# Diagonal blocks gathered by ScalarE, and one 128-partition block transpose in place of four, in a recurrence's inverse

## The chip, the cores and the metric

The kernel runs on one core of a Trainium2 chip. The metric is device time in microseconds of one execution. Six kinds of rows appear in its profile: PE and PEld (TensorE's matmuls and weight loads), DVE (VectorE), ACT (ScalarE), POOL (GpSimd) and SP (the engine that issues most DMAs). Each engine works through its own queue in order; an instruction whose inputs are not ready holds up everything behind it on that engine.

## The reference

One layer of a hybrid model over 2048 tokens of width 1024, with 256 context tokens ahead of them, in float32: a norm with modulation, a projection to 4544 columns, two token mixers over those columns, an output projection, and a layer of 16 experts. The mixer that matters here is RWKV-7, run forwards and backwards over 8 heads of 64:

```python
def step(S, inp):
    r_t, w_t, k_t, v_t, a_t, b_t = inp
    sa = jnp.einsum('bhvk,bhk->bhv', S, a_t)
    S = S * w_t[:, :, None, :] + sa[..., None] * b_t[:, :, None, :] + v_t[..., None] * k_t[:, :, None, :]
    return S, jnp.einsum('bhvk,bhk->bhv', S, r_t)
```

The other mixer is a retention with a fixed decay; its columns are the projection `h @ w_in` over the first 2560 columns.

## The kernel before

The kernel does not walk the recurrence token by token. It cuts the tokens into chunks of 64. Inside a chunk the term `sa` of each token depends on those of the tokens before it; written out, that is a triangular system of 64 by 64 per head and chunk, whose inverse is needed. A `Job` is 256 tokens (four chunks, 8 heads) in one direction: 9 blocks times 2 directions are 18 jobs, forward and backward in turn.

How a job goes, by the names in the code:

- `loads`, `decays`, `decays_b` fetch its rows and multiply in the running decays (DVE and ACT).
- `product(m, q)`, four times: matmuls on PE into PSUM (`pA`), and DVE multiplies by a mask into `ab` (the triangular matrices) and `rb`. Partitions 0 to 63 of `ab` hold one half of the chunks (q = 0), 64 to 127 the other (q = 1); the free axis has 16 matrices of 64 columns for each q.
- `corners(q)` (lines 970 to 980): each 64 by 64 triangle is seen as two 32 by 32 diagonal blocks and one corner block. ACT copies the corner into `lo`; DVE transposes the diagonal blocks into `xp`. A DVE block transpose turns each 32 by 32 block by itself, so what lies on one partition as (16 matrices, 32 columns) comes out with the matrix index along the free axis. There is one transpose per diagonal block, each of 32 partitions and 1024 elements (every element is written twice, by a broadcast).
- `inverses`: POOL inverts all the 32 by 32 blocks at once by back substitution, 31 steps of a multiply (line 997) and an add (line 1000) on `dm`.
- `spread(q)` (lines 1002 to 1010): DVE transposes the inverted blocks back, from `dm` into the two diagonal places of `Y[d]`, and one of the two once more into `Dn` (tile `D` in the profile).
- `solve`: matmuls in eight steps. Its third step multiplies `lo` by `Dn` and ACT copies the product over the other half of `Dn`; its fourth multiplies that by `y` and ACT copies it into the corner of `y`; the later steps apply `y`.
- `chain`: the four chunks one after the other, each with a matmul into `pC`, a DVE add into `uv`, a matmul, a DVE add and multiply into the next state `z`, and matmuls for the outputs (`yo`).

The order is written out by hand: every matmul, DVE and ACT instruction of this stage keeps its program order. The loop of lines 1186 to 1203 has 12 slots per job. In slot i it issues one step of the chain of the job before, then a share of the retention columns' matmuls as filler (`fill_slot`, 9.1 per slot; 24 of them make one column tile in the single PSUM bank `pr`, which ACT then reads into `ru`), then the steps of the job's own solve (its third and fourth are in slots 6 and 7), and last what is prepared for it or for the next job: `product` of the next job in slots 4 to 7, `corners` of the next job in slot 7, `inverses` from slot 8 to its slot 16, and `spread` in slot 17, that is in slot 5 of the job's own turn. POOL also issues the column loads `rh` in the same queue as the inverses; SP issues the other loads.

`xp`, `lo`, `D`, `ab` and `dm` have one buffer each. Nearly all instructions carry line 126 in the profile (the helper that records them), so the rows below go by tile names; `hi` in a row of this stage is another name on the same memory (the decays, the masks).

Of the kernel before, what the change touches and what calls it, by code (L numbers as in the profile page):

```python
# [8 lines left out]
F32 = mybir.dt.float32  # L9
# [75 lines left out]
def body(ctx: ExitStack, tc, a, out, scratch, stop=None, only=None):  # L85
# [53 lines left out]
    vec, act, pool = Ordered(nc.vector), Ordered(nc.scalar), Ordered(nc.gpsimd)  # L139
# [728 lines left out]
    def rwkv():  # L868
        with ExitStack() as es:
            one = es.enter_context(tc.tile_pool(name="s1", bufs=1, reuse_waits="tile"))  # L870
# [6 lines left out]
            Dn = one.tile([128, 16, 32], F32, name="D")  # L877
# [28 lines left out]
            class Job:  # L906
# [62 lines left out]

                def corners(self, q):  # L970

                    if "xp" not in self.__dict__:
                        self.xp = one.tile([128, 1024], F32, name="xp")
                        self.lo = one.tile([128, 16, 32], F32, name="lo")
                    r, b = slice(64 * q + 32 * self.d, 64 * q + 32 * self.d + 32), 32 - 32 * self.d
                    act.copy(out=self.lo[r], in_=self.ab[r, q].rearrange("p m h t -> p (m h) t")[:, :, b:b + 32])
                    for b in range(2):
                        r = slice(64 * q + 32 * b, 64 * q + 32 * b + 32)
                        src = self.ab[r, q].rearrange("p m h (y t) -> p y t (m h)", y=2)[:, b]
                        vec.transpose(out=self.xp[r], in_=self.rev(src)[:, :, None, :].to_broadcast([32, 32, 2, 16]))  # L980

                def inverses(self, j0, j1):

# [15 lines left out]
                            tc.keep_in_program_order(x)  # L999
                        eng.tensor_add(dm[:, 0:j, j // 2:], dm[:, 0:j, j // 2:], tv)  # L1000

                def spread(self, q):

                    d, y = self.d, Y[self.d]
                    dm = self.dm.rearrange("p (s r) -> p r s", r=16)
                    for b in (1 - d, d):
                        r, t = slice(64 * q + 32 * b, 64 * q + 32 * b + 32), slice(32 * b, 32 * b + 32)
                        o = y[r, :, t].rearrange("p u t -> p t u")
                        vec.transpose(out=self.rev(o), in_=dm[r, :, ::-1] if d else dm[r])
                    vec.transpose(out=Dn[r].rearrange("p u c -> p (u c)"), in_=y[r, :, t])  # L1010

                def values(self):
                    self.uv = one.tile([128, 2, 2, W], F32, name="uv", bufs=2)
# [136 lines left out]
            def ahead(job):  # L1150

                r = {i: [] for i in range(20)}
                r[0].append(job.loads)
                r[AT_LOAD] += [job.loads_b, job.decays]
                r[AT_DEC].append(job.decays_b)
                for i, (m, q) in enumerate((m, q) for m in job.o2 for q in job.o2):
                    r[AT_PROD + i].append(lambda m=m, q=q: job.product(m, q))
                for i, q in enumerate(job.o2):
                    r[AT_DIAG[i]].append(lambda q=q: job.corners(q))
                for i in range(len(INV) - 1):  # L1160
                    r[AT_INV + i].append(lambda i=i: job.inverses(INV[i], INV[i + 1]))
                for q in range(2):
                    r[AT_SPREAD[q]].append(lambda q=q: job.spread(q))
                return r

            rate = [0.0]
# [1 line left out]
            def fill_slot(x):  # L1168
                rate[0] += x
                n = int(rate[0])  # L1170
                rate[0] += fill(n) - n

            side = ahead(jobs[0])
            jobs[0].loads()
            jobs[0].loads_b()
# [10 lines left out]
            for j, job in enumerate(jobs):  # L1186
                nxt = ahead(jobs[j + 1]) if j + 1 < len(jobs) else {}
                job.values()
                solve = job.solve()
                for i in range(SLOTS):  # L1190
                    next(chain, None)
                    if i == AT_COPY:
                        job.copies_a()
                    fill_slot(F_SLOT * F_BEAT[(SLOTS * j + i) % len(F_BEAT)])
                    for _ in range(SOLVE.count(i)):
                        next(solve)
                    if 1 <= i <= 2:
                        for q in job.o2:
                            job.copies_b(job.o2[i - 1], q)
                    for f in side.get(SLOTS + i, []) + nxt.get(i, []):  # L1200
                        f()
                side = nxt
                chain = job.chain()
# [34 lines left out]
                nc.gpsimd.tensor_sub(g.wl[:, k, js], raw, g.wh[:, k, js].bitcast(F32))  # L1238
                yield

    AT_LOAD, AT_DEC, AT_PROD, AT_DIAG, AT_INV, AT_SPREAD, AT_COPY = 2, 3, 4, (7, 7), 8, (17, 17), 5
    INV = (31, 28, 25, 22, 19, 16, 12, 8, 4, 0)
    SOLVE = (2, 3, 6, 7, 8, 9, 10, 11)
    J_VEC = 0
# [919 lines left out]
```

## Time and profile before

| | |
|---|---|
| median of 3 runs | 3589.23 us (3582.62 to 3590.91) |
| the profiled execution | 3576.91 us |
| its span, first to last instruction | 3574.9 us |
| PE busy | 3197.0 us (89%) |
| DVE busy | 2271.5 us (64%) |
| ACT busy | 1380.3 us (39%) |
| POOL busy | 1216.9 us (34%) |
[...]

The durations and waits come from the one profiled execution. Busy shares are averages over stages with different limits, so the rows below are taken from the stage in which the change lies. A number in square brackets at the end of a timeline row is how long the engine had stood idle before it, and what ended that.

### The profile page before, as it was taken

The numbers are of one execution on the slowest core, as the hardware profiler recorded it, in microseconds if no ns is written. First come the engines' busy times: TensorE is split into PE (matmuls) and PEld (weight loads), VectorE is DVE, ScalarE is ACT, GpSimd is POOL, SyncE is SP. The second block draws the span as 40 slices with busy tenths as digits, with TensorE's granted clock in tenths as the row PEclk, the third lists the DMA queues.
The fourth block names the chain that finished last, engine by engine and source line by source line (L and its number), as shares of the span: only waits on it lengthen the run. The fifth ranks groups of instructions, "written<-read, shape, count | busy, mean of one in ns | idle before, by whom it ended". The sixth has DMA issues, their size and how long they took to land. (4 is left out here: it accounts for less than half of the span.)

```text
span 3574.9 us, 74834 instructions
## 1 busy us (share of the span) xinstructions
PE 3197.0 (89%) x30786; PEld 2783.1 (78%) x30786; DVE 2271.5 (64%) x3904; ACT 1380.3 (39%) x2468; POOL 1216.9 (34%) x1969
## 2 busy tenths in 40 slices
PE   6999999788888888999978888849999999998888
PEld 4898889666767777777766777639999999998787
DVE  6676745566657556546427777675655665567765
ACT  4645343222222223333333333324444444444443
POOL 2010101464554554453634444220000000017774
PEclk9999999888999999999978988869999999999999
DMA  8886763545445456455457544236766666678885
GB/s 259 258 250 197 220 191 119 177 147 163 151 146 181 149 180 195 145 167 168 159 187 245 184 164 163 91 118 212 224 199 211 214 204 207 204 233 302 284 297 192
DMA packets 468221, 692.80 MB, mean 194 GB/s; under 512 B 30232, under 2 KB 345253, under 8 KB 457001
## 3 DMA queue, kind: packets, MB, share of 16 engines
q1 hardware_dynamic: 441480, 550.62, 47.4%
q0 software_dynamic: 25824, 136.36, 12.5%
q8 instruction: 242, 3.96, 0.4%
q10 hardware_dynamic: 576, 1.05, 0.1%
q14 instruction: 99, 0.80, 0.1%
HBM read 534.56 MB, written 153.37 MB: 192 GB/s over the span
## 5 line engine op out<-in xcount | busy, mean ns | idle before, releaser
L126 DVE TENSOR_TENSOR ewl<-ewr,ewh 128x1024 fp32r<-128x1024 f32 x376 | 474.3, 1303 | 250.2 <-ACT ewh L126 250.2
L126 PE MATMUL pr<-rwh,rh 128*128 128x512 f32 x1344 | 484.6, 428 | 35.7 <-ACT ru L126 16.9
L126 ACT CAST ewh<-ewr 128x1024 fp32r<-128x1024 f32 x376 | 374.2, 1046 | 0.5 <-DMA ewr<-in_w_down_dram 0.5
L126 PEld LDWEIGHTS pr<-rwh,rh 128*128 128x128 f32 x1344 | 268.7, 202 | 101.9 <-ACT ru L126 18.6
L126 PE MATMUL pu<-hi,whi 128*128 128x258 f32 (+1 forms) x1104 | 327.2, 296 | 5.0 <-ACT hi L406 5.0
L126 PE MATMUL pu<-lo,whi 128*128 128x258 f32 (+1 forms) x1104 | 315.9, 286 | 4.0 <-DVE lo L407 2.3
L126 PE MATMUL pu<-hi,wlo 128*128 128x258 f32 (+1 forms) x1104 | 314.4, 285 | 0.0
L997 POOL TENSOR_TENSOR dtmp<-xp,dm 128x126 f32<-128x126 f32 (+22 forms) x558 | 248.1, 445 | 186.8 <-DVE xp L126 146.9
L126 PE MATMUL pg<-xh,ewh 128*128 128x256 f32 x1024 | 293.0, 286 | 0.0
L126 PE MATMUL pu<-xh,ewh 128*128 128x256 f32 x1024 | 289.9, 283 | 0.8 <-DVE sg L126 0.8
L126 PE MATMUL pg<-xh,ewl 128*128 128x256 f32 x1024 | 290.4, 284 | 0.0
L126 PE MATMUL pg<-xl,ewh 128*128 128x256 f32 x1024 | 290.3, 284 | 0.0
L126 PE MATMUL pu<-xl,ewh 128*128 128x256 f32 x1024 | 289.9, 283 | 0.0
L126 PE MATMUL pu<-xh,ewl 128*128 128x256 f32 x1024 | 289.8, 283 | 0.0
L126 PE MATMUL pr<-rwl,rh 128*128 128x512 f32 x672 | 282.4, 420 | 4.4 <-DVE rwl L126 4.4
L1000 POOL TENSOR_TENSOR dm<-dm,dtmp 128x126 f32<-128x126 f32 (+22 forms) x558 | 269.0, 482 | 43.0
L126 PEld LDWEIGHTS pu<-hi,whi 128*128 128x128 f32 (+1 forms) x1104 | 208.2, 189 | 14.6 <-ACT hi L406 5.8
L126 PE MATMUL po<-ewh,hh 128*128 128x512 f32 x512 | 212.2, 414 | 0.0
L126 PEld LDWEIGHTS pu<-lo,whi 128*128 128x128 f32 (+1 forms) x1104 | 208.0, 188 | 5.2 <-DVE lo L407 3.2
L126 PEld LDWEIGHTS pu<-hi,wlo 128*128 128x128 f32 (+1 forms) x1104 | 208.6, 189 | 2.8 <-issue 2.2
L126 PE MATMUL po<-ewh,hl 128*128 128x512 f32 x512 | 203.6, 398 | 0.0
L126 PE MATMUL po<-ewl,hh 128*128 128x512 f32 x512 | 202.9, 396 | 0.0
(525 smaller groups left out, 7720.0 us busy)
## 6 DMA issues: line engine op xcount, KB each, us to landing
rh<-s_hT POOLq DMA_DIRECT2D x84, 1024.0 KB, 6.0
ewr<-in_w_gate_dram SPq DMA_DIRECT2D x64, 1024.0 KB
ewr<-in_w_up_dram SPq DMA_DIRECT2D x64, 1024.0 KB
ewr<-in_w_down_dram SPq DMA_DIRECT2D x64, 1024.0 KB
s_ret<-ru SPq DMA_DIRECT2D x84, 256.0 KB
wraw<-in_w_in_dram SPq DMA_DIRECT2D x156, 128.0 KB
bk<-s_bk SPq DMA_DIRECT2D x17, 1024.0 KB
mw<-in_w_mod_dram SPq DMA_DIRECT2D x128, 128.0 KB
```

Source lines behind the costliest of these rows:

```text
L126: return lambda *args, **kw: tc.keep_in_program_order(op(*args, **kw))
L997: x = eng.tensor_mul(tv, ma[:, j, 0:j, None].to_broadcast(sh), dm[:, j:j + 1, j // 2:].to_broadcast(sh))
L1000: eng.tensor_add(dm[:, 0:j, j // 2:], dm[:, 0:j, j // 2:], tv)
```

## The change

`corners` is still called for each q. ACT now copies both diagonal blocks of that q into `Dn`, so that all four blocks of the 128 partitions lie side by side in one tile of (128, 16, 32), and on the second call DVE transposes them into `xp` in one instruction of 128 partitions. `spread` is called once: one transpose of 128 partitions turns `dm` into a tile `yc` (a second use of the memory and the name of `xp`), one more turns `yc` into `Dn`, and ACT copies the four blocks from `yc` into their places in `y`. Both are called in the same slots as before.

```diff
 def corners(self, q):
-    if "xp" not in self.__dict__:
+    first_ = "xp" not in self.__dict__
+    if first_:
         self.xp = one.tile([128, 1024], F32, name="xp")
         self.lo = one.tile([128, 16, 32], F32, name="lo")
-    r, b = slice(64 * q + 32 * self.d, 64 * q + 32 * self.d + 32), 32 - 32 * self.d
-    act.copy(out=self.lo[r], in_=self.ab[r, q].rearrange("p m h t -> p (m h) t")[:, :, b:b + 32])
+    ab = self.ab[:, q].rearrange("p m h t -> p (m h) t")
     for b in range(2):
         r = slice(64 * q + 32 * b, 64 * q + 32 * b + 32)
-        src = self.ab[r, q].rearrange("p m h (y t) -> p y t (m h)", y=2)[:, b]
-        vec.transpose(out=self.xp[r], in_=self.rev(src)[:, :, None, :].to_broadcast([32, 32, 2, 16]))
+        act.copy(out=Dn[r], in_=ab[r, :, 32 * b:32 * b + 32])
+    if not first_:
+        src = self.rev(Dn.rearrange("p u t -> p t u"))
+        vec.transpose(out=self.xp, in_=src[:, :, None, :].to_broadcast([128, 32, 2, 16]))
+    r, b = slice(64 * q + 32 * self.d, 64 * q + 32 * self.d + 32), 32 - 32 * self.d
+    act.copy(out=self.lo[r], in_=ab[r, :, b:b + 32])
...
-def spread(self, q):
+def spread(self):
     d, y = self.d, Y[self.d]
     dm = self.dm.rearrange("p (s r) -> p r s", r=16)
+    yc = one.tile([128, 1024], F32, name="xp")[:, 0:512].rearrange("p (u t) -> p u t", t=32)
+    vec.transpose(out=self.rev(yc.rearrange("p u t -> p t u")), in_=dm[:, :, ::-1] if d else dm)
+    vec.transpose(out=Dn.rearrange("p u c -> p (u c)"), in_=yc)
     for b in (1 - d, d):
-        r, t = slice(64 * q + 32 * b, 64 * q + 32 * b + 32), slice(32 * b, 32 * b + 32)
-        o = y[r, :, t].rearrange("p u t -> p t u")
-        vec.transpose(out=self.rev(o), in_=dm[r, :, ::-1] if d else dm[r])
-    vec.transpose(out=Dn[r].rearrange("p u c -> p (u c)"), in_=y[r, :, t])
+        for q in range(2):
+            r, t = slice(64 * q + 32 * b, 64 * q + 32 * b + 32), slice(32 * b, 32 * b + 32)
+            act.copy(out=y[r, :, t], in_=yc[r])
...
-for q in range(2):
-    r[AT_SPREAD[q]].append(lambda q=q: job.spread(q))
+r[AT_SPREAD].append(job.spread)
...
-AT_LOAD, AT_DEC, AT_PROD, AT_DIAG, AT_INV, AT_SPREAD, AT_COPY = 2, 3, 4, (7, 7), 8, (17, 17), 5
+AT_LOAD, AT_DEC, AT_PROD, AT_DIAG, AT_INV, AT_SPREAD, AT_COPY = 2, 3, 4, (7, 7), 8, 17, 5
```

## Rows read from the trace of the kernel before

**Rows 1.** Recurrence stage: length, busy us of PE, PEld, DVE, ACT, POOL, granted clock, DMA.

```profile
640.00:1820.00 1180.00, 1040.87 (x13934) 846.38 (x13934) 706.60 (x1061) 351.19 (x634) 591.04 (x1266) 0.93 0.50 161
```

**Rows 2.** Waits of PE, 640 to 1820 us: total, times, longest.

```profile
PE pC L126 <- DVE uv L126: 68.3, 30, 4.4
PE pD L126 <- DVE D L126: 19.4, 11, 2.6
PE pr L126 <- ACT ru L126: 17.7, 6, 7.7
PE pr L126 <- DMA rh<-s_hT: 12.6, 5, 4.5
```

**Rows 3.** Timeline of DVE in one job: start, length, operation, idle before.

```profile
1145.28 2.25 DVE L126 STREAM_TRANSPOSE y<-dm 32x512 f32<-32x512 f32 x2
...
1163.95 0.75 DVE L126 TENSOR_TENSOR ab<-pA,hi 128x256 f32<-128x256 f32 x2 [2.61 <-PE pA L126]
1164.62 0.74 DVE L126 TENSOR_TENSOR rb<-pA,hi 128x256 f32<-128x256 f32 x2
1165.29 7.82 DVE L126 STREAM_TRANSPOSE xp<-ab 32x1024 f32<-32x1024 f32 x4
1173.14 0.77 DVE L126 TENSOR_TENSOR uv<-pC,uv 64x256 f32<-64x256 f32 x2
```

**Rows 4.** Timeline of PE in the same job.

```profile
1169.52 1.15 PE L126 MATMUL pD<-f,y 64*64 64x64 f32 x32
1173.96 0.69 PE L126 MATMUL pC<-uv,hi 128*64 128x64 f32 x16 [3.29 <-DVE uv L126]
```

**Rows 5.** Timeline of PE: first, largest and last wait behind an xp batch.

```profile
772.63 1.12 PE L126 MATMUL pC<-uv,hi 128*64 128x64 f32 x16 [4.42 <-DVE uv L126]
...
1238.91 0.80 PE L126 MATMUL pr<-rwh,rh 128*128 128x512 f32 x1 [5.51 <-DVE rsb L126]
...
1758.40 0.69 PE L126 MATMUL pC<-uv,hi 128*64 128x64 f32 x16 [1.00 <-DVE uv L126]
```

**Rows 6.** Timeline of PE: a job that waits for both halves of D.

```profile
1015.31 0.21 PE L126 MATMUL pD<-D,lo 32*32 32x32 f32 x2 [1.89 <-DVE D L126]
1018.11 1.91 PE L126 MATMUL pD<-D,lo 32*32 32x32 f32 x62 [2.58 <-DVE D L126]
```

**Rows 7.** Windows behind waits of PE, columns as in rows 1.

```profile
1018.11:1026.11 8.00, 8.00 (x103) 6.76 (x103) 4.21 (x12) 1.15 (x2) 0.25 (x2) 0.57 0.01 2
1238.91:1246.91 8.00, 8.00 (x51) 6.33 (x53) 1.93 (x4) 0.00 (x0) 6.83 (x17) 0.72 0.05 16
1512.76:1520.76 8.00, 8.00 (x112) 6.46 (x116) 0.85 (x2) 1.89 (x5) 6.70 (x19) 1.00 0.42 121
```

**Rows 8.** Groups of instructions, 620 to 1810 us: busy us, mean ns, idle before.

```profile
L126 DVE STREAM_TRANSPOSE xp<-ab 32x1024 f32<-32x1024 f32 x72 | 141.7, 1968 | 0.9
L126 DVE STREAM_TRANSPOSE y<-dm 32x512 f32<-32x512 f32 x72 | 79.2, 1100 | 12.5 <-POOL dm L1000 11.1
L126 DVE TENSOR_TENSOR ab<-pA,hi 128x256 f32<-128x256 f32 x144 | 54.4, 418 | 88.0 <-PE pA L126 87.5
L126 DVE TENSOR_TENSOR uv<-pC,uv 64x256 f32<-64x256 f32 x132 | 49.9, 416 | 90.8 <-PE pC L126 89.8
L126 DVE STREAM_TRANSPOSE D<-y 32x512 f32<-32x512 f32 x36 | 25.3, 703 | 1.2
L126 ACT COPY lo<-ab 32x512 f32<-32x512 f32 x36 | 22.2, 617 | 14.0 <-DVE ab L126 13.0
```

**Rows 9.** Timeline of ACT in the job of rows 3.

```profile
1162.88 1.18 ACT L126 COPY y<-pD 32x512 f32<-32x512 f32 x2 [6.19 <-PE pD L126]
1164.08 1.27 ACT L126 COPY lo<-ab 32x512 f32<-32x512 f32 x2
1167.05 0.60 ACT L126 ACTIVATE ru<-pr 128x512 f32<-128x512 f32 x1 [1.70 <-PE pr L126]
```

**Rows 10.** Waits of POOL, 640 to 1820 us.

```profile
POOL dtmp L997 <- DVE xp L126: 146.9, 18, 16.1
```

## The prediction

> **What bounds the kernel now.** I read four views, from the whole to the single wait. First the busy time by stage. The recurrence with the retention columns beside it runs from about 640 to 1820 us, a third of the span, and there the matmul unit (PE) is busy 1040.87 of 1180 us, VectorE (DVE) 706.60, ScalarE (ACT) 351.19, GpSimd (POOL) 591.04 [rows 1]. The reader is to see that PE is the nearest thing to a bound, but idle for 139 us. The change touches nothing outside this stage, so what it can win or lose is looked for here.
>
> Second, who ends PE's idle time: the uv adds on DVE 68.3 us, DVE's transposes into D 19.4, ru on ACT 17.7, the column loads 12.6 [rows 2]. DVE is thus the engine that PE waits for, although it is only 60% busy: what counts is the order of its queue at a few places.
>
> Third, these places, in one job (rows of 1144 to 1176 us). DVE does four xp transposes back to back, 7.82 us from first start to last end; queued behind them is the uv add of the chain, at 1173.14, and PE waits 3.29 us for it [rows 3, 4]. Going through PE's waits over 0.3 us in the whole stage and comparing their times with the xp transposes, I find 15 of them that end right behind an xp batch (14 on uv, one on rsb), 39.9 us together; the first is 4.42, the largest 5.51, the last 1.00 [rows 5]. The other uv waits follow the decay work in slots 2 and 3 and stay. Waits for D are 10 by the same list, 19.2 us; the usual pattern is a first matmul that starts with the first half of D, and 2.58 us lost until the second half is there [rows 6].
>
> Fourth, the granted clock just after these waits. Where PE had been idle 2.2 us or more before it went on, the next 8 us mostly show a mean clock of 0.5 to 0.8; behind the waits of 1.5 us or less it is 1.00 (0.57 after 2.58 us of idling, 0.72 after 5.51, but 1.00 after 1.40) [rows 7]. [...]
>
> **The change, part by part.** Per job (18 jobs), with durations of [rows 8] unless another group is named.
>
> DVE loses four xp transposes of 1968 ns, four of dm into y of 1100 and two of y into D of 703: 7.87 + 4.40 + 1.41 = 13.7 us. It gains one xp transpose of 128 partitions by 1024, one of dm and one into D, both 128 by 512. No transpose over 128 partitions is in the trace. Lower end: the same time as the 32-partition one of the same length, 1.97 + 1.10 + 0.70 = 3.8 us. Upper end: four times that, 15.1 us, if the blocks of the four quadrants went one after the other. I take the lower end, as the nearest row that compares partition counts is an elementwise one: 64 by 256 takes 416 ns and 128 by 256 takes 418. [...]
>
> ACT gains four copies of ab into D and four of the transposed blocks into y, all 32 by 512. The nearest row is lo from ab, the same shape, 617 ns: 4.9 us per job, 89 us in all, on an engine that is idle for 829 of 1180 us [rows 1].
>
> *Corners (slot 7).* New order: ACT copies D, D, lo for the first q, then D, D, lo for the second; DVE's single transpose waits for the fifth copy. In the job shown, ACT ends its y copies at 1164.06 [rows 9]. The first q is ready long before; three copies end at 1165.9, the next two, whose ab is there at 1164.70 [rows 3], at 1167.15. DVE idles from 1165.36 to then, transposes until 1169.1 instead of 1173.1, and the uv add runs 4.0 us earlier. PE's 15 waits shrink by up to 4.0 us: all go but 0.4 of the 4.42 and 1.5 of the 5.51. Gain 38 us. What is late next at that place is PE's own work: in the job shown its matmuls before the wait end at 1170.67 [rows 4], after the uv add.
>
> *Spread (slot 5).* D is complete after 1.10 + 0.70 = 1.8 us instead of 4 x 1.10 + 2 x 0.70 = 5.8 (from 1145.28 in the job shown [rows 3]). The second-half waits go entirely; the three first-half waits (2.08, 1.89, 1.01) shrink by 1.1 at most, since the first half came after 2.9 us. About 2 us stays. Gain 17 us. The y copies are needed only one slot later and end 3.5 us after DVE's start.
>
> *Clock.* After nine of the 15 waits and five of the D waits the clock was below 1.00. Summing (1 - clock) times 8 us over these windows gives 17 + 15 = 32 us. With the waits gone this comes back unless something else stops PE in the same places; I take three quarters, 24 us.
>
> *Costs.* ACT works in order. In slot 7 what stands behind the four extra copies is ru (1167.05 [rows 9]) and the uv copies: they move by up to 2.5 us, but the PSUM bank of ru is next written in the following slot's fill, mostly after that. In slot 5 the y copies make ACT wait for DVE; what is queued behind is a ru of the next fill and the D copies. A ru comes once in 24 filler matmuls, 9.1 to a slot, so 0.38 per slot; a slot lasts 1180 / 18 / 12 = 5.5 us and ACT is held for about 3.5 of it, so about one job in four has a ru there, moved by 1.7 us on average. PE waits at once for a late ru only at the start of the next column. I take 6 us for both. Below nothing there is a gain too: POOL starts its inverses 4 us earlier (it waits 146.9 us for xp now [rows 10]), which may bring forward the column loads it issues; at most the 12.6 us of [rows 2]. Against it I put 8 us of new waits elsewhere, since PE reaches the next dependency sooner.
>
> Sum: 38 + 17 + 24 - 6 - 8 = 65 us. The profiled execution took 3576.91 us, so a like one takes 3512. The median of the runs is 12.3 us above it; the same saving from 3589.23 gives 3524.
>
> **The rivals.**
>
> *ACT becomes the late one.* Its queue has ru, casts of weights and the y copies ahead of the five copies that DVE now waits for, so DVE's stall eats half the gain: xp only 2 us earlier. Then the 15 waits give 25.6 instead of 38, the clock some 15 instead of 24, D 12, and ru stalls cost 12: 41 us, 3549. For it: the cast group of column changes; against it: in all but one of the 16 batches from 764 us on, ACT's rows show it idle, at its y copies or at the lo copies when ab ended, as in [rows 9].
>
> *The time comes back elsewhere.* If the chain from one state to the next, or the loads, set the pace, PE waits as long at other places: about 3585. For it: the other uv waits, 68.3 less the 34.4 of the fourteen above (some 34 us), are on the same chain. Against it: PE's queue is in order, its work is not changed, and between these waits it is busy without a break.
>
> *Slower: the wide transpose works its quadrants in turn.* Place: DVE, slots 7 and 5. Price: xp is done 1.8 + 7.9 us after rb, 1.8 later than now, on 16 batches 29 us; D is complete after 7.2 us, not 5.8, on the seven jobs that wait for it now 10 us; some 10 for the clock behind longer waits and 6 for ACT. 3589 + 55 = 3644. It decides from the point where the wide xp transpose takes more than 6.1 us (7.9 less the 1.8 of the new wait). The equal times of 64 and 128 partitions speak against it.
>
> *The change does little of what it says*: that would show as DVE's transposes still 32 partitions wide; the diff leaves no room for it, so it has no chance of its own.
>
> **How the numbers follow.** Forecast 0.68 (its own range 3495 to 3545), ACT late 0.18, time comes back 0.08, slower 0.06. The range: downward, everything saved with the whole clock and the loads, 38 + 17 + 32 + 12, gives 3490; upward, the ACT case with half its clock gain and some new waits, 3568. A difference within 0.2% (7 us) can't be told from none here. Faster: the forecast, the ACT case and a fifth of the third, 0.88; same: most of the third, 0.06; slower 0.06.
>
> **What would show it.** In the changed kernel's rows: 18 transposes of 128 by 1024 at about 1.97 us, 36 of 128 by 512 at 1.10 and 0.70; 144 more ACT copies of about 0.6 us; PE's waits on uv down from 68 to about 35 us and on D from 19 to about 2; POOL's wait for xp down by some 70 us; the stage's mean clock up from 0.93 to 0.95 or more; the recurrence ending some 65 us earlier and everything behind it unchanged. Wrong it would be if the wide transposes take several times as long, if PE's waits on ru grow by more than 20 us, or if the clock stays where it is although the waits are gone.

## The result, and the profile after

The changed kernel takes 3490.78 us (median of 4 runs, 3487.07 to 3494.43) against 3590.07 before on the same chip: ratio 0.9732, 95% interval 0.9717 to 0.9748, or 99 us less. The forecast was 3524, 65 us less; the measured time lies 1 us inside the lower end of the range (3490), and outside the forecast's own 3495 to 3545.

Its profiled execution took 3491.34 us, 85.6 us less than the 3576.91 of the profiled execution before. This pair of executions does not show the other 13 us: the execution profiled before was a quick one of its kernel, 13 us under the median of runs that spread from 3572 to 3597 us over the whole study. The terms of the sum are therefore compared with 85.6.

Busy time by stage, from 640 us to the last output copy of the recurrence and from there to the end, columns as in [rows 1]; first the kernel before:

```profile
640.00:1844.20 1204.20, 1057.46 (x14153) 860.25 (x14152) 711.66 (x1071) 362.13 (x655) 607.04 (x1279) 0.93 0.50 160
1844.20:3574.90 1730.70, 1550.66 (x12232) 1395.48 (x12232) 1145.77 (x1870) 719.01 (x1205) 533.35 (x601) 0.93 0.64 209
```

and the changed kernel:

```profile
640.00:1751.10 1111.10, 1023.25 (x14151) 834.01 (x14150) 535.88 (x945) 445.14 (x796) 604.54 (x1278) 0.96 0.55 173
1751.10:3489.50 1738.40, 1556.37 (x12232) 1399.28 (x12232) 1146.81 (x1870) 719.33 (x1205) 534.40 (x602) 0.93 0.64 209
```

The recurrence is 93.1 us shorter. PE's idle time in it (length less busy) falls from 146.7 to 87.9 us, by 58.9; its busy time falls by 34.2 us for the same matmuls, at a mean granted clock of 0.96 of full speed and not 0.93. What follows is 7.7 us longer in this execution.

PE's waits in the recurrence (total, times, longest), to be read beside [rows 2]; first those of the kernel before, up to its last output copy, where they are not the lines of [rows 2]:

```profile
PE pC L126 <- DVE uv L126: 71.0, 33, 4.4
PE pC L126 <- DVE z L126: 9.3, 4, 4.4
PE pr L126 <- DVE rsb L126: 6.0, 2, 5.5
PE pA L126 <- DVE bk L126: 4.8, 5, 1.8
PE pC L126 <- ACT yo L126: 3.2, 1, 3.2
```

and the changed kernel:

```profile
PE pC L126 <- DVE uv L126: 36.4, 20, 4.3
PE pr L126 <- ACT ru L126: 15.4, 7, 5.5
PE pC L126 <- DVE z L126: 10.5, 4, 5.0
PE pr L126 <- DMA rh<-s_hT: 9.5, 5, 3.8
PE pA L126 <- DVE bk L126: 7.5, 7, 2.6
PE pC L126 <- ACT yo L126: 3.4, 1, 3.4
PE pr L126 <- DVE rsb L126: 1.3, 2, 0.8
PE pD L126 <- DVE D L126: 0.9, 1, 0.9
```

uv, rsb and D together lose 57.8 us: all but 1 us of the fall of the idle time.

The new instructions, by tile (ns: shortest, median, longest), to [rows 8]:

```profile
L126 ACT COPY y<-xp x72: 601/617/622, 682.5 to 1700.4; 32x512 f32<-32x512 f32 x72
L126 DVE STREAM_TRANSPOSE xp<-D x18: 1932/2001/2099, 640.1 to 1660.3; 128x1024 f32<-128x1024 f32 x18
L126 DVE STREAM_TRANSPOSE xp<-dm x18: 1078/1118/1172, 681.3 to 1693.9; 128x512 f32<-128x512 f32 x18
L126 DVE STREAM_TRANSPOSE D<-xp x18: 711/711/715, 682.5 to 1695.1; 128x512 f32<-128x512 f32 x18
```

At the median, a transpose of 128 partitions takes 2.00, 1.12 and 0.71 us where one of 32 took 1.97, 1.10 and 0.70 [rows 8]. The job that [rows 3, 4, 9] show, in the changed kernel, DVE:

```profile
1103.79 0.76 DVE L126 TENSOR_TENSOR ab<-pA,hi 128x256 f32<-128x256 f32 x2 [2.64 <-PE pA L126]
1104.46 0.74 DVE L126 TENSOR_TENSOR rb<-pA,hi 128x256 f32<-128x256 f32 x2
1107.08 1.98 DVE L126 STREAM_TRANSPOSE xp<-D 128x1024 f32<-128x1024 f32 x1 [1.87 <-ACT D L126]
1109.09 0.77 DVE L126 TENSOR_TENSOR uv<-pC,uv 64x256 f32<-64x256 f32 x2
```

ACT:

```profile
1102.71 1.18 ACT L126 COPY y<-pD 32x512 f32<-32x512 f32 x2 [6.19 <-PE pD L126]
1103.91 1.25 ACT L126 COPY D<-ab 32x512 f32<-32x512 f32 x2
1105.17 0.62 ACT L126 COPY lo<-ab 32x512 f32<-32x512 f32 x1
1105.81 1.24 ACT L126 COPY D<-ab 32x512 f32<-32x512 f32 x2
1107.07 0.62 ACT L126 COPY lo<-ab 32x512 f32<-32x512 f32 x1
1107.71 0.60 ACT L126 ACTIVATE ru<-pr 128x512 f32<-128x512 f32 x1
```

and PE:

```profile
1107.71 0.63 PE L126 MATMUL pC<-z,ptt 64*64 64x64 f32 x13
1108.36 0.69 PE L126 MATMUL pr<-ru,rt 128*64 128x64 f32 x16
1108.88 0.64 PE L126 MATMUL pr<-ru,rkt 128*64 128x64 f32 x16
1109.44 1.15 PE L126 MATMUL pD<-f,y 64*64 64x64 f32 x32
1110.52 0.69 PE L126 MATMUL pC<-uv,hi 128*64 128x64 f32 x16
```

DVE now waits 1.87 us for ACT and is through with xp 3.9 us earlier after rb than before; the uv add ends at 1109.86 and PE takes it at 1110.52 without a wait, where it had waited 3.29 us. Look also at ru. In the kernel before, ACT stood idle for 1.70 us ahead of it and ended it at 1167.65 [rows 9], and PE took it 0.79 us later:

```profile
1167.88 0.63 PE L126 MATMUL pC<-z,ptt 64*64 64x64 f32 x13
1168.44 0.69 PE L126 MATMUL pr<-ru,rt 128*64 128x64 f32 x16
```

In the changed kernel ACT has no gap above 0.02 us from 1102.71 on, ru ends at 1108.31, and PE starts on it at 1108.36. These 0.05 us are no slack: wherever the list of waits has PE waiting for ru, it starts 0.05 or 0.06 us after the end of ru. PE begins 0.65 us after the start of the last 13 matmuls on z and not 0.56 as before, so it is 0.09 us late. The four new copies, 2.5 us, have used up the gap and the 0.79 us behind it; the experiments come back to this.

### The profile page after: what moved, and what is told of

Read it like the earlier page. It is cut to its first block, busy times and chain, and to the rows that moved or that the text cites. A ratio compares the mean times of both kernels' runs of the same rounds, so it can differ in the third digit from the quotient of the medians.

```text
span 3489.5 us, 74870 instructions
## 1 busy us (share of the span) xinstructions
PE 3171.3 (91%) x30786; PEld 2763.1 (79%) x30786; DVE 2096.4 (60%) x3778; ACT 1465.9 (42%) x2612; POOL 1215.6 (35%) x1969
## 5 line engine op out<-in xcount | busy, mean ns | idle before, releaser
L126 PE MATMUL pr<-rwh,rh 128*128 128x512 f32 x1344 | 473.2, 419 | 25.4 <-ACT ru L126 14.3
L126 PEld LDWEIGHTS pr<-rwh,rh 128*128 128x128 f32 x1344 | 261.7, 197 | 88.9 <-ACT ru L126 16.5
L1001 POOL TENSOR_TENSOR dtmp<-xp,dm 128x126 f32<-128x126 f32 (+22 forms) x558 | 254.4, 456 | 165.3 <-DVE xp L126 118.9
```

Of the source, the lines that this page charges most:

```text
L126: return lambda *args, **kw: tc.keep_in_program_order(op(*args, **kw))
L1001: x = eng.tensor_mul(tv, ma[:, j, 0:j, None].to_broadcast(sh), dm[:, j:j + 1, j // 2:].to_broadcast(sh))
```

## The experiments

Theory A is that of the prediction: PE idles because the chain's uv add, and D, stand behind transposes in DVE's queue, and long waits cost clock as well (0.57 of full speed in the 8 us behind 2.58 us of idling [rows 7]). Each experiment's time is compared with the kernel before on its own chip. The changed kernel, run again below, shares a chip only with the runs of all eight copies twice, of the copies into y on DVE and of the decays alone; a difference from it in the other runs is between chips, and the ratios say how far it holds.

**The two parts alone.** The changed `corners` with the old `spread`, and the reverse.

```diff
 (first)  corners as changed;  def spread(self, q): as before, called for each q
 (second) corners as before;   def spread(self): as changed, called once
```

> Changed corners (ACT copies, one transpose into xp), old spread. Theory A (what counts is DVE time queued ahead of the chain's uv add): PE's waits behind the xp batches (39.9 us before) fall to under 3 us, the ten waits for D stay at about 19 us, the clock gives back some 17 us: about 55 us faster than before, 3535. Theory B (any DVE work removed in the stage counts alike, 5.9 of the 9.9 us per job removed here): 59 us faster, and the waits for D shrink too. Theory C (the extra ACT copies have a price that the whole change hides): under 40 us faster, with waits on ru above 25 us.

> Old corners, changed spread (two wide transposes, ACT copies into y). Theory A: the waits for D fall from 19.4 to about 2 us, the waits behind the xp batches stay at about 40 us, some 15 us of clock: about 32 us faster, 3558. Theory B: 4.0 of 9.9 us of DVE work per job, 40 us faster. Theory C: the y copies, queued behind DVE, hold ru back: under 20 us faster.

Corners alone: 3534.52 us, ratio 0.986 (0.9837 to 0.9884), 52 us faster. Spread alone: 3548.87, 0.9895 (0.987 to 0.9919), 37 us faster. Together 89 of some 99. PE's waits for uv and D with corners alone:

```profile
PE pC L126 <- DVE uv L126: 36.4, 20, 4.3
PE pD L126 <- DVE D L126: 17.5, 10, 2.6
```

and with spread alone:

```profile
PE pC L126 <- DVE uv L126: 70.7, 33, 4.4
PE pD L126 <- DVE D L126: 2.3, 2, 1.4
```

Each part removes its own wait and leaves the other's. Less DVE work as such (theory B) would have eased both. Theory C, a hidden price of the copies, expected smaller gains and falls for the copies as they are.

**The queue, or POOL's earlier start?** Both follow from an earlier xp. Eight more DVE transposes into a scratch area, behind or ahead of the one into xp, part them.

```diff
+for _ in range(8):                                    # ahead, in the second kernel
+    vec.transpose(out=first.e[:, 0:512], in_=Dn.rearrange("p u t -> p (u t)"))
 vec.transpose(out=self.xp, in_=src[:, :, None, :].to_broadcast([128, 32, 2, 16]))
+for _ in range(8):                                    # behind, in the first
+    vec.transpose(out=first.e[:, 0:512], in_=Dn.rearrange("p u t -> p (u t)"))
```

> The changed kernel with eight more DVE transposes of 128 by 512 (0.71 us each, 5.7 us per job) into a scratch area right BEHIND the transpose into xp. POOL gets xp as early as in the changed kernel; the chain's uv add is late again, by 5.7 us, some 1.7 us later than in the kernel before. Theory A: PE's waits behind these batches come back, 40 to 65 us, and the clock falls with them: 60 to 95 us slower than the changed kernel, about 3560. Rival POOL (the gain comes from the inverses and the loads that POOL issues starting earlier): under 15 us slower than the changed kernel, about 3500.

> The same eight transposes AHEAD of the transpose into xp: the uv add is as late as with the eight behind, and POOL gets xp 5.7 us later too. Theory A: within 10 us of the kernel with the eight behind. Rival POOL: at least 30 us slower than that one, about 3540 against 3500. Both together: each counts in part.

Behind: 3569.56 us, ratio 0.9953 (0.9939 to 0.9966), 79 us slower than the changed kernel although POOL has xp as early (DVE waits 29.8 us for ACT ahead of the 18 transposes into xp, against 29.7). Ahead: 3587.67, 1.0008 (0.9993 to 1.0022), 18 us more. The stage and PE's waits with the eight behind:

```profile
640.00:1838.60 1198.60, 1055.08 (x14157) 858.64 (x14157) 633.89 (x1093) 446.98 (x797) 598.79 (x1280) 0.93 0.51 161
```

```profile
PE pC L126 <- DVE uv L126: 91.0, 34, 6.4
PE pD L126 <- DVE D L126: 0.9, 1, 0.9
```

and PE's waits for D with the eight ahead, with its two longest:

```profile
PE pD L126 <- DVE D L126: 11.4, 3, 7.3
```

```profile
688.30 1.91 PE L126 MATMUL pD<-D,lo 32*32 32x32 f32 x64 [7.31 <-DVE D L126]
...
747.63 0.60 PE L126 MATMUL pD<-D,lo 32*32 32x32 f32 x15 [3.19 <-DVE D L126]
```

5.9 us of DVE work per job ahead of the uv add, that is 106 us in all, brings back 54.6 us of waits on uv, and with them the slower clock, 0.93 and not 0.96: PE is busy 1055.08 us and not 1023.25. The loss splits as the change's gain did: 55.7 us idle and 31.8 busy here, 58.9 and 34.2 there. POOL's start counts too, but less: of the 18 us, 10.5 are waits for D, nearly all in the first two jobs. My 10 us bound for the difference was too tight.

**The price of ACT's copies.** All eight done twice, then each place alone.

```diff
-act.copy(out=Dn[r], in_=ab[r, :, 32 * b:32 * b + 32])
+for _ in range(2):
+    act.copy(out=Dn[r], in_=ab[r, :, 32 * b:32 * b + 32])   # all eight; corners only
...
-act.copy(out=y[r, :, t], in_=yc[r])
+for _ in range(2):
+    act.copy(out=y[r, :, t], in_=yc[r])                     # all eight; spread only
```

> The changed kernel with each of its eight new ACT copies per job done twice (4.9 us more ACT time per job, 89 us in all, at the same two places; DVE's transpose into xp waits two to four copies longer, 1.2 to 2.5 us). Theory A with a price on ACT as I put it (6 us for the eight copies): 5 to 15 us slower than the changed kernel. Theory A with ACT free as the trace of the changed kernel suggests (PE's waits on ru fell from 17.7 to 15.4): within 5 us. Rival (ACT is the new limiter): over 30 us slower, waits on ru above 30 us.

> Only the four copies of ab into D done twice (2.5 us more ACT per job in slot 7, DVE's transpose into xp 1.2 to 2.5 us later). All eight twice cost 52 us, with PE's waits on ru up from 15 to 40 us, most of them next to the xp transposes. If ACT's cover ends in slot 7: at least 35 of the 52 us, about 3530, waits on ru above 30 us. If the two places share it: 20 to 30 us. If slot 5 is the tight place: under 15 us.

> Only the four copies into y done twice (2.5 us more ACT per job in slot 5). If ACT's cover ends in slot 7: under 15 us slower than the changed kernel, about 3495 to 3505, waits on ru about 20 us or less. If slot 5 is the tight place: 35 us or more.

All eight: 3542.52 us, ratio 0.988 (0.9859 to 0.99), 52 us slower than the changed kernel on the same chip, with 40.1 us of waits on ru. Here I was wrong, the rival right. Corner copies: 3531.39, 0.984 (0.9823 to 0.9856), 36 to 41 us slower, by the ratios or by the medians. Copies into y: 3504.28, 0.9766 (0.9731 to 0.98), 9 to 13 us, with an interval that overlaps that of the changed kernel (0.9718 to 0.9762): not clear of the scatter. PE's waits with the corner copies twice:

```profile
PE pC L126 <- DVE uv L126: 44.0, 24, 4.2
PE pr L126 <- ACT ru L126: 31.1, 12, 5.7
PE pr L126 <- DMA rh<-s_hT: 16.9, 5, 8.1
```

and rows of ACT, PE and DVE at the place that the timeline above shows:

```profile
1129.12 0.60 ACT L126 ACTIVATE ru<-pr 128x512 f32<-128x512 f32 x1
1129.77 0.69 PE L126 MATMUL pr<-ru,rt 128*64 128x64 f32 x16 [2.62 <-ACT ru L126]
1128.49 1.93 DVE L126 STREAM_TRANSPOSE xp<-D 128x1024 f32<-128x1024 f32 x1 [4.48 <-ACT D L126]
```

The four copies that the change put into slot 7 fill ACT's slack at this place; the next four don't fit, and PE waits 2.62 us for ru. That is not their only price: DVE's transpose into xp waits for the same copies, 4.48 us here and not 1.87, and 75.6 us over the 18 jobs and not 29.7, so the uv add comes later again. PE idles 31.1 us more in this stage than in the changed kernel: 15.7 are waits on ru, 10.6 on uv and rsb and 7.4 on rh, with 2.4 less elsewhere. Its busy time grows by 10.6. So the first four copies cost little that shows, and the same again costs some 40 us, half of the added idle time as waits on ru. How much of it would remain if xp were not late as well, no run here shows.

**Copies into y on DVE.**

```diff
-act.copy(out=y[r, :, t], in_=yc[r])
+vec.tensor_copy(y[r, :, t], yc[r])
```

> The changed kernel with the four copies into y done by DVE behind the transpose into D, not by ACT. Theory A: DVE gets some 2 us per job in slot 5 ahead of the masks of the next product and of the uv add of slot 6, where it has slack of 4 us against the kernel before: within 8 us of the changed kernel. If any DVE work in the stage counts (theory B, 99 us for 9.9 us per job): 15 to 20 us slower.

3504.53 us, but its five runs spread from 3484.71 to 3510.67; ratio 0.9781 (0.9758 to 0.9805) against 0.974 (0.9718 to 0.9762). The profiled run was the quickest of them and has a recurrence as long as the changed kernel's. This one settles nothing.

**The changed kernel again.**

> The changed kernel itself, for the comparison on the same chip and for a second profile: 3485 to 3500; the recurrence within 5 us of the first profile, and the output stage, 9 us longer there than in the one profile of the kernel before, within 5 us of it if the change caused that, or anywhere in 525 to 540 if it is chance.

3490.92 us. Its recurrence ends at 1753.2 us, its span is 3484.0, so 1730.8 us follow: as long as in the kernel before (1730.7). The 7.7 us that the first profile lost there are chance. Against the 11 runs of the kernel before on this chip (median 3584.45) the gain is 93.5 us, ratio 0.974 (0.9718 to 0.9762).

```profile
640.00:1753.20 1113.20, 1023.30 (x14150) 834.17 (x14148) 535.27 (x945) 444.41 (x794) 604.01 (x1279) 0.96 0.54 172
```

**What is left.** The remaining uv waits stand behind the decays; and DVE still waits for ACT ahead of xp.

```diff
 (decays)  -r[AT_LOAD] += [job.loads_b, job.decays]
           +r[AT_LOAD].append(job.loads_b)
           +r[AT_LOAD - 1].append(job.decays)
 (gather)  +side_ = first.e[:, 0:512].rearrange("p (u t) -> p u t", t=32)   # in place of Dn, in corners
           -AT_DIAG = (7, 7)
           +AT_DIAG = (6, 7)
```

> The changed kernel with the next job's decays (scans, exponentials, the multiply of ar) issued in slot 1 and not 2, so that the uv add of slot 3 no longer stands behind them. If the 33.7 us of uv waits that remain are DVE queue time of that work: they fall to under 10 us, and with the clock the kernel is 25 to 45 us faster than the changed one, about 3455. Rival (the decays then wait for their loads, which are issued in slot 0, and hold DVE as long): no faster than 5 us, or slower.

> The changed kernel with the blocks gathered in a free piece of the decays' scratch area instead of D, so that the first q's three ACT copies can be issued in slot 6, not 7. DVE's wait for ACT ahead of xp (29.7 us in all) should fall to about 15 us, and ACT is held 1.9 us less in slot 7. If the waits on ru are what is left of the price of the copies: 5 to 15 us faster than the changed kernel. If ACT's wait for the mask multiply of slot 6 takes its place: no gain, or up to 15 us slower.

> The same, with the decays of the next job issued in slot 1 too (alone 21 us faster than the changed kernel). If the two act on different waits they add: 3455 to 3465. If they meet on ACT: no better than the decays alone, 3470.

Decays earlier: 3469.65 us, ratio 0.969 (0.9666 to 0.9714), the fastest of the study, 21 us faster than the changed kernel and less than the 25 to 45 expected. Gather earlier: 3485.93, 0.9708 (0.9689 to 0.9727); DVE's wait for ACT ahead of xp fell from 29.7 to 13.2 us and PE's for ru from 15.4 to 10.6, but the interval overlaps that of the changed kernel, so a gain is not shown. Both: 3479.68, 0.9698 (0.9679 to 0.9716), no better than the decays alone. PE's waits with the decays earlier:

```profile
PE pD L126 <- ACT f L126: 13.8, 11, 2.5
PE pA L126 <- DVE bk L126: 11.3, 9, 4.0
PE pC L126 <- DVE uv L126: 4.0, 6, 0.9
```

The uv waits went as expected, 36.4 to 4.0. But the exponentials now stand in slot 1 on ACT, ahead of the PSUM copies f of the second slot, and PE waits 13.8 us for those; with both edits it is 16.9 on f and 15.7 on bk. Of the 32.4 us of uv waits that went, only 10.4 show as less idle time (77.4 us against 87.9); of what came back, the waits on f are the largest part. Why the two edits don't add is open: against the decays alone the waits on ACT's f grew by 3.1 us, those on DVE's bk by 4.4.

## Why the prediction was right, and where a size was off

- *The bound.* Right: DVE's queue at two places. Idle time fell by the waits named, within 1 us, and putting the queue back (eight transposes behind xp) put the waits back.
- *The wide transposes.* Right, at the lower end of the bounds: 2.00, 1.12 and 0.71 us at the median against 1.97, 1.10 and 0.70. The slower rival hung on this alone and is excluded.
- *Corners, 38 us of waits.* uv and rsb fell by 39.3. DVE's wait for ACT, put at 1.8 us per job, is 29.7 / 18 = 1.65.
- *Spread, 17 us.* D fell by 18.5.
- *Clock, 24 us.* Mis-sized: PE's busy time fell by 34.2, all that the sum over the windows had given (32) and not three quarters of it. The caution had no row behind it: PE's other waits fell by 1.3 us in all, so nothing took the place of those that went. The reading behind the term holds as a sum and not for each wait: in the same trace of the kernel before, after waits of 2.29 to 2.66 us at 937, 982, 1204 and 1637 us, the next 8 us show a clock of 1.00.
- *Costs, 14 us.* The term that failed most. "I take 6 us for both" and "8 us of new waits": the waits other than uv, rsb and D changed by -2.3 (ru), -3.1 (rh), +1.2 (z), +2.7 (bk) and +0.2 (yo), 1.3 us less in all and not 14 more. That ACT's copies are cheap was right only up to their number: twice as many cost 52 us. A flat price for the copies was the wrong form; a slack is used up. The prediction looked for it in the PSUM bank of ru; in the job shown what counted was PE's matmul on ru. The rows of the kernel before have that slack: 1.70 us of gap ahead of ru and 0.79 behind it, for 2.5 us of copies.
- *POOL.* I gave its earlier start no gain. Of the signs named, this one failed: POOL's wait for xp fell from 146.9 [rows 10] to 118.9 us, by 28 and not some 70 (its wait ahead of dm, for the job before to be read, fell from 101.8 to 62.7). The two kernels with eight transposes put it at up to 18 us for 5.9 us per job; the change, which moved xp by about 4, may owe it part of the waits for D in the first jobs. That part was not isolated.
- *The base.* The saving was worked out on an execution 13 us quicker than the median and subtracted from the median; the 99 us measured between medians hold some of the scatter of the kernel before (93.5 us on another chip). That the time lies inside the range at all, by 1 us, is luck: the lower end was to be reached by the whole clock and 12 us of loads, and the waits for rh fell by 3.1. Execution against execution 65 us were forecast and 85.6 measured. The stage itself adds up: 39.3 + 18.5 + 34.2 and the 1.3 of the other waits, against 93.1 us; this execution then lost 7.7 us behind it.

The rival "ACT becomes the late one" did not happen, but it was nearer than its chance said: in the job above PE comes to ru 0.09 us late, with no slack left. "The time comes back elsewhere" did not happen either; the edit of the decays shows how it looks when it does.

## What to carry to other kernels

Look not at the busy share of an engine but at what stands in its queue ahead of the one instruction that the bound engine needs next; four small instructions that one wide one can replace are worth most there (here four transposes of 7.82 us became one of 1.98, and corners alone gained 52 us). Count a long wait twice where the granted clock falls behind it: here 59 us less idling came with 34 us less busy time. And before moving work to an idle engine, read the gaps of that engine at the very place: the copies here cost almost nothing while the gap held them, and the next four some 40 us, in part because they also held back the transpose that waits for them.

## What the runs showed of the hardware

DVE's transpose of 128 partitions by 1024 takes 2.00 us and that of 32 partitions 1.97, so in these rows four times the partitions cost 2%; the stride of the reads went from 256 to 128 bytes at the same time. With both sides contiguous, 512 elements take 0.71 us, with both strided 1.12. PE's same 14,150 matmuls of this stage were busy 1057 us with 147 us of idle time among them, 1023 with 88, and 1055 when 56 us of idling were put back, to 144, at a mean granted clock of 0.93, 0.96 and 0.93 of full speed. PE kept the order of its queue: at 1015 and 1018 us in the kernel before it stood idle 1.89 and 2.58 us for the halves of D [rows 6], with matmuls on an rh it had been using since 1011.09 further back in its queue; they went on at 1023.01.
